# Wider dense products and single-head attention steps in a two-layer hybrid decoder trunk on one NeuronCore

## The chip, the core and the metric

The kernel runs on one core of a Trainium2 chip. The metric is device time in microseconds (us) of one execution of the whole program. TensorE multiplies: it loads a stationary tile and streams a moving tile past it into PSUM, of which a bank here is one tile of 128 x 512 fp32. VectorE and ScalarE do the elementwise work and read PSUM, GpSimd (POOL) does small scalar chains on SBUF, and SyncE (SP) issues most DMA transfers. Every engine runs its own queue of instructions in order.

## What is computed

Two residual layers over 256 tokens of width 2048, with 256 rows of memory; all in fp32. In outline, from the reference:

```python
mem_n = rms_norm(mem, mem_norm_gain)
for i in range(2):
    h = rms_norm(x, norm_gain[i])
    if i == 0:   # 8 NSA heads (3 branches), 4 differential heads, 4 memory heads
        a_q, a_kv, a_g, a_z, b_q, b_k, b_v, b_z, m_q, m_z = split(h @ even_w_in)
        y = concat(nsa(a_q, a_kv, a_g) * silu(a_z), diff(b_q, b_k, b_v) * silu(b_z),
                   memory(m_q, mem_n @ mem_w_kv[0]) * silu(m_z))
    else:        # 12 heads over the top-k tokens of a 16-head indexer, 4 memory heads
        c_q, c_k, c_v, i_q, i_k, i_w, c_z, m_q, m_z = split(h @ odd_w_in)
        y = concat(dsa(c_q, c_k, c_v, i_q, i_k, i_w) * silu(c_z),
                   memory(m_q, mem_n @ mem_w_kv[1]) * silu(m_z))
    x = x + y @ w_out[i]
```

NSA has a compressed branch (15 blocks of 32 tokens through a small MLP), a branch over selected blocks (all of them at this length) and a window branch; each is a masked softmax of its own, and a sigmoid gate weighs them.

## The kernel before

**Numbers in two parts.** Every fp32 operand of a large product is kept as a high part (rounded to fp32r by ScalarE) and a low part (the rest, a VectorE subtraction), and a product is three passes: high x high, low x high, high x low (`passes`). Products of small weight keep plain fp32.

**The weight stream.** `CHUNKS` (L28 to L48) lists the dense products in the order in which their weights are read. A chunk of up to 256 columns comes in four pieces of four k tiles, a wider one in eight pieces of two (`k_tiles`): a piece is 512 KB, 128 x 1024. `emit_raw` loads it through SP's queue up to four pieces ahead; `emit_split` makes `whi` (ScalarE, L189) and `wlo` (VectorE, L190), two pieces ahead, in three buffers each.

**Two kinds of dense product.** `dense_nat` (L221) puts tokens on partitions: the activations are stationary, the weights move, per k tile 3 passes x 2 token blocks. With 256 columns both token blocks share one bank; only memk0 and memk1 are 512 wide. `dense_T` (L247) puts columns on partitions: the weights are stationary, the 256 tokens move, per k tile and column tile three products of 256:

```python
for j, (a, w) in enumerate(((hi, wh), (lo, wh), (hi, wl))):
    T.matmul(outs[ct], w[:, k_, ct * P:(ct + 1) * P], a[:, kt, :], ...)
```

Dense results sit in the pool `pd`, three tiles of one bank; scores in `pS` (two banks), transposes in `pT` (two), attention outputs in `pO` (one).

**The order of the work.** Start: memory keys and values of both layers (memk, memv, memw) beside the norm of x, which generators feed in between (`run_background`, so many steps per weight piece). Layer 0: cmp0, cmp1 and the compression MLP `compress_all` (background, 0.85 steps per piece, its weights through the buffers `raw`), keys and values (ks, vs), then for each of four head pairs `nsa_pair` (L784) and beside them `diff_q`/`diff_pair` (L869, L880), then memory attention (L485), the gates z0 to z7 (`gated`, L952) and the output projection o0 to o7 (L975). Layer 1 (L1000 on): the indexer (ikw, iq), its top-k on VectorE (L1063 to L1074), keys and values, six pairs of DSA heads (L1093 to L1133), memory attention, gates y0 to y7, projection p0 to p7. A framework makes the engines' queues from this program: it takes instructions whose inputs it expects to be ready in the order of their priority, which is the order in the code unless a priority is given, and adds the waits.

In `nsa_pair` two heads share their products with the values (L855 to L863): per branch the first 256 token columns of both heads move as 512, the last 128 of both as 256. `sumsq_heads` takes one ScalarE square with accumulation per token block and head. `gated` reads the gate's product from PSUM and the attention output `oT`, and splits the product of the two into the halves of y.

## Time and profile before

| | |
|---|---|
| three runs | 977.37, 979.40, 981.41 us; median 979.4 us |
| profiled execution | span 976.5 us from first to last instruction; the page lists no further time for it |
| TensorE products | 967.4 us busy (99% of the span), 7801 products |
| TensorE weight loads | 943.2 us busy (97%) |
| VectorE | 642.6 us (66%) |
| ScalarE | 528.7 us (54%) |
| GpSimd | 158.9 us (16%) |
| DMA | 182.40 MB, mean 187 GB/s |

Busy time says in how much of the span an engine had an instruction under way; products overlap one another in TensorE's pipeline, so its busy time can include waits shorter than a product's own duration. The spacing of products (start to start) is what one of them costs.

### The profile page before, as it was taken

The page shows a single profiled execution, that of the slowest core. Times are in us where ns is not written, and L with a number is a line of the kernel's source. Part 1 is how long each engine was busy: PE and PEld are TensorE (multiplying, and loading weights), DVE is VectorE, ACT ScalarE, POOL GpSimd, SP SyncE. Part 2 cuts the span into 40 slices and gives each one's busy share as a digit, 9 for nine tenths or more (in the row PEclk, how much of TensorE's full clock was granted, in tenths as well). Part 3 has the DMA queues.
Part 4 walks back from the last instruction along what each step waited for, and adds up shares of the span by engine and source line. Part 5 has one row for each costly group of instructions (what it writes and reads, how often), then busy time and mean ns, then how long its engine had stood idle before and what let it go on. Part 6 is the DMA issues. An engine that isn't in the chain of part 4 may idle for free.

```text
span 976.5 us, 19895 instructions
## 1 busy us (share of the span) xinstructions
PE 967.4 (99%) x7801; PEld 943.2 (97%) x7801; DVE 642.6 (66%) x1153; ACT 528.7 (54%) x1072; POOL 158.9 (16%) x499
## 2 busy tenths in 40 slices
PE   8999999999999999999999999999999999999998
PEld 6989988899999999999999999999999999999998
DVE  5777854667778766675666667779667667665453
ACT  6756533456676666564454455554466666443332
POOL 0144102223113102200000030021243310000000
PEclk9999999999999999999999999999999999999999
DMA  8765768844444444545677674445654545556772
GB/s 310 253 209 191 238 226 300 286 167 151 143 146 136 133 160 151 171 154 167 205 253 238 192 234 153 148 130 178 194 153 148 156 146 152 171 177 213 218 232 91
DMA packets 55901, 182.40 MB, mean 187 GB/s; under 512 B 6352, under 2 KB 8400, under 8 KB 55808
## 3 DMA queue, kind: packets, MB, share of 16 engines
q1 hardware_dynamic: 54160, 176.77, 55.9%
q0 software_dynamic: 1216, 4.05, 1.3%
q8 instruction: 61, 1.00, 0.4%
q10 hardware_dynamic: 432, 0.32, 0.1%
q14 instruction: 32, 0.26, 0.1%
HBM read 175.88 MB, written 5.24 MB: 185 GB/s over the span
## 4 chain that ended last, share of the span: by engine, by line
PE 96%; DVE 2%; DMA 1%; issue 0%; ACT 0%; SPq 0%; DVEq 0%
PE dn L241 47%; PE dn L262 39%; PE pt L339 2%; PE S L836 1%; PE S L698 1%; PE S L1054 1%; DMA raw<-in_W 1%; PE S L501 1%; DVE wlo L190 1%; PE po L514 1%; PE po L1131 0%; PE S L1117 0%; PE S L908 0%; PE pt L508 0%; DMA raw<-in_w 0%; DVE lo_h L272 0%
## 5 line engine op out<-in xcount | busy, mean ns | idle before, releaser
L190 DVE TENSOR_TENSOR wlo<-raw,whi 128x1024 fp32r<-128x1024 f32 (+3 forms) x305 | 365.0, 1197 | 222.5 <-ACT whi L189 221.0
L189 ACT ACTIVATE whi<-raw 128x1024 fp32r<-128x1024 f32 (+3 forms) x305 | 316.6, 1038 | 315.1 <-PE dn L262 149.4
L241 PE MATMUL dn<-wlo,hi_h 128*128 128x256 f32 (+2 forms) x1024 | 214.3, 287 | 0.0
L241 PE MATMUL dn<-whi,lo_h 128*128 128x256 f32 (+2 forms) x1024 | 213.1, 286 | 0.0
L241 PE MATMUL dn<-whi,hi_h 128*128 128x256 f32 (+2 forms) x1024 | 211.2, 285 | 0.0
L241 PEld LDWEIGHTS dn<-wlo,hi_h 128*128 128x128 f32 x1024 | 161.5, 191 | 5.1 <-issue 3.9
L262 PE MATMUL dn<-hi_h,wlo 128*128 128x256 f32 x576 | 163.6, 284 | 0.7 <-DVE wlo L190 0.7
L262 PE MATMUL dn<-lo_h,whi 128*128 128x256 f32 x576 | 163.7, 284 | 0.0
L262 PE MATMUL dn<-hi_h,whi 128*128 128x256 f32 x576 | 163.6, 284 | 0.0
L241 PEld LDWEIGHTS dn<-whi,lo_h 128*128 128x128 f32 x1024 | 161.4, 191 | 2.1 <-issue 1.2
L241 PEld LDWEIGHTS dn<-whi,hi_h 128*128 128x128 f32 x1024 | 160.7, 191 | 1.5 <-issue 0.8
L262 PE MATMUL dn<-hi_y,whi 128*128 128x256 f32 x512 | 145.0, 283 | 0.0
L262 PE MATMUL dn<-lo_y,whi 128*128 128x256 f32 x512 | 144.9, 283 | 0.0
L262 PE MATMUL dn<-hi_y,wlo 128*128 128x256 f32 x512 | 144.9, 283 | 0.0
L262 PEld LDWEIGHTS dn<-hi_h,wlo 128*128 128x128 f32 x576 | 109.9, 191 | 1.4 <-DVE wlo L190 0.9
L262 PEld LDWEIGHTS dn<-lo_h,whi 128*128 128x128 f32 x576 | 110.1, 191 | 0.0
L262 PEld LDWEIGHTS dn<-hi_h,whi 128*128 128x128 f32 x576 | 110.0, 191 | 0.0
L262 PEld LDWEIGHTS dn<-hi_y,whi 128*128 128x128 f32 x512 | 97.4, 190 | 0.0
L262 PEld LDWEIGHTS dn<-lo_y,whi 128*128 128x128 f32 x512 | 97.4, 190 | 0.0
L262 PEld LDWEIGHTS dn<-hi_y,wlo 128*128 128x128 f32 x512 | 97.4, 190 | 0.0
L372 ACT ACTIVATE E<-E,mn 128x128 f32<-128x128 f32 (+1 forms) x88 | 40.1, 458 | 22.3 <-DVE mn L371 19.5
L241 PE MATMUL dn<-whi,hi_mem 128*128 128x256 f32 (+1 forms) x192 | 47.2, 322 | 2.3 <-ACT hi_mem L430 2.3
(342 smaller groups left out, 1205.7 us busy)
## 6 DMA issues: line engine op xcount, KB each, us to landing
raw<-in_W SPq DMA_DIRECT2D x287, 512.0 KB, 3.6
raw<-in_w SPq DMA_DIRECT2D x16, 512.0 KB, 4.4
raw<-in_W SPq DMA_DIRECT2D x8, 336.0 KB, 3.3
raw<-in_W SPq DMA_DIRECT2D x8, 280.0 KB, 3.3
xs<-in_xT SPq DMA_DIRECT2D x8, 256.0 KB, 5.9
ld<-in_xT SPq DMA_DIRECT2D x8, 256.0 KB, 4.2
x1d<-x POOLq DMA_DIRECT2D x8, 256.0 KB, 4.2
ld<-x1d SPq DMA_DIRECT2D x8, 256.0 KB, 4.2
```

The lines of the kernel that those rows point to most:

```text
L189: state["last"] = (A.activation(hi[:, c], r[:, c], AF.Copy), V.tensor_tensor(lo[:, c], r[:, c], hi[:, c].bitcast(F32), OP.subtract))
L190: V.tensor_tensor(lo[:, c], r[:, c], hi[:, c].bitcast(F32), OP.subtract))
L241: T.matmul(outs[tb], a[:, kt, tb * P:(tb + 1) * P], w[:, k_, :], start=(kt == 0 and j == 0 and (n > 256 or tb == 0)), stop=(kt == KT - 1 a ...
L262: T.matmul(outs[ct], w[:, k_, ct * P:(ct + 1) * P], a[:, kt, :], start=(kt == 0 and j == 0 and (apart or ct == 0)), stop=(kt == KT - 1 and ...
L339: T.transpose(ps[:, b, :], src[:, b * P:(b + 1) * P], ident)
L372: A.activation(E, E, AF.Exp, bias=mn, scale=-1.0, accum_out=sm)
L501: T.matmul(ps_s[:, tb, :], a[:, i, tb * P:(tb + 1) * P], b[:, h, :], start=(j == 0), stop=(j == 2))
L514: T.matmul(po[:, i, :], a[:, mt, h * P:(h + 1) * P], b[:, mt, :], start=(mt == 0 and j == 0), stop=(mt == 1 and j == 2))
L698: T.matmul(ph[l4 * 32:(l4 + 1) * 32, :], blks[j][:, l, :, :].rearrange("p g c -> p (g c)"), wt[:, l4, :], start=(l < 4), stop=(l >= 28), t ...
L836: T.matmul(ps_s[:, :, :n], a[:, i, tb * P:(tb + 1) * P], b[:, g, :, :n], start=(j == 0), stop=(j == 2))
L1054: T.matmul(ps_s[:, :, :n], x[:, b, tb * P:(tb + 1) * P], z[:, :, :n], start=(j == 0), stop=(j == 2))
```

## The change

Dense products of 512 columns wherever two chunks of 256 lay side by side; `dense_T` moves the high and the low part of an activation in one product of 512 columns, into a bank of its own per column tile; attention is written as generators of one head each, of which two run in turn, so many steps per weight piece; a head's output and its gate are multiplied in whichever order they come (`Gated`); memory and differential attention come ahead of NSA; PSUM is two dense tiles of two banks, three banks for the heads and one for preparing queries and keys. The core of the diff:

```diff
-CHUNKS = [("memk0", "mem0", 0, 512), ("memv0", "mem0", 512, 256), ("memw0", "mem0", 768, 256),
...
+CHUNKS = [("memk0", "mem0", 0, 512), ("memv0", "mem0", 512, 512), ("memk1", "mem1", 0, 512), ("memv1", "mem1", 512, 512),
+          ("mq0", "even", 5656, 512), ("cmp0", "even", 1024, 256), ("cmp1", "even", 1280, 256),
+          ("bq", "even", 3608, 512), ("bk", "even", 4120, 512), ("bv", "even", 4632, 512),
+          ("ks", "even", ((1536, 128), (2048, 128), (1664, 128), (2176, 128)), 512),
+          ("vs0", "even", ((1792, 128), (2304, 128), (2560, 24)), 280), ("vs1", "even", ((1920, 128), (2432, 128)), 256),
+          ("aq0", "even", 0, 512), ("aq1", "even", 512, 512)]
...
+CHUNKS += [(f"iq{_i}", "odd", 2560 + 512 * _i, 512) for _i in range(2)]
+CHUNKS += [("mq11", "odd", 5456, 256), ("ck", "odd", 1536, 512), ("cv", "odd", 2048, 512)]
+CHUNKS += [(f"cq{_i}", "odd", 512 * _i, 512) for _i in range(3)]
...
-        pd = ctx.enter_context(tc.tile_pool(name="pd", bufs=3, space=bass.MemoryType.PSUM))
-        pS = ctx.enter_context(tc.tile_pool(name="pS", bufs=2, space=bass.MemoryType.PSUM))
-        pT = ctx.enter_context(tc.tile_pool(name="pT", bufs=2, space=bass.MemoryType.PSUM))
-        pO = ctx.enter_context(tc.tile_pool(name="pO", bufs=1, space=bass.MemoryType.PSUM))
+        pd = ctx.enter_context(tc.tile_pool(name="pd", bufs=2, space=bass.MemoryType.PSUM))
+        pS = ctx.enter_context(tc.tile_pool(name="pS", bufs=3, space=bass.MemoryType.PSUM))
+        pT = pO = pS
...
+        PER_PIECE = 0.9
...
         def run_background():
+            run_attention()
...
+        def step():
+            while len(lines) < 2 and waiting and over.issuperset(waiting[0][2]):
+                lines.append(waiting.pop(0))
+            if lines:
+                line = lines.pop(0)
+                with tc.high_priority(100000):
+                    end = next(line[1], StopIteration) is StopIteration
+                if end:
+                    over.add(line[0])
+                else:
+                    lines.append(line)
+
+        def attended(*numbers):
+            while not over.issuperset(numbers):
+                step()
+
+        def run_attention():
+            steps["due"] += steps["per_piece"]
+            while steps["due"] >= 1:
+                steps["due"] -= 1
+                step()
...
+            ps = pd.tile([P, 2, 512], F32, name="dn")
...
-                    for j, (a, w) in enumerate(((hi, wh), (lo, wh), (hi, wl))):
-                        T.matmul(outs[ct], w[:, k_, ct * P:(ct + 1) * P], a[:, kt, :],
-                                 start=(kt == 0 and j == 0 and (apart or ct == 0)), stop=(kt == KT - 1 and j == 2),
-                                 skip_group_check=True)
+                    cs = slice(ct * P, (ct + 1) * P)
+                    T.matmul(ps[:, ct, :], wh[:, k_, cs], act.both(kt), start=(kt == 0), stop=False, skip_group_check=True)
+                    T.matmul(ps[:, ct, S:], wl[:, k_, cs], act[kt, 0, :], start=False, stop=(kt == KT - 1),
+                             skip_group_check=True)
                 run_background()
-            return ps
+            return ps[:, :, :S], ps[:, :, S:]
...
+            A.activation(junk, v[:, :, off:off + nh * hd], AF.Square)
+            V.tensor_reduce(ssq.rearrange("p (t h) -> p t h", t=2), junk.rearrange("p t (h d) -> p t h d", h=nh), AX.X, OP.add)
...
+        def prep_bank():
+            return pS.tile([P, 512], F32, name="pp", bufs=1)
...
+        class Gated:
...
+            def put(self, c, n, first, second):
+                for seen, run in itertools.groupby(range(n), lambda k: c + k in self.seen):
+                    run = list(run)
+                    k = slice(run[0], run[-1] + 1)
+                    (second if seen else first)(self.oT[:, c + k.start:c + k.stop, :], k)
+                    (self.ready if seen else self.seen).update(c + i for i in run)
+                self.flush()
+
+            def attention(self, c, n, po):
+                self.put(c, n, lambda t, k: A.activation(t, po[:, k], AF.Copy),
+                         lambda t, k: V.tensor_tensor(t, po[:, k], t, OP.mult))
+
+            def release(self, *quarters):
+                self.free |= set(quarters)
+                self.flush()
+
+            def flush(self):
+                for c in range(0, KT, 2):
+                    if {c, c + 1} <= self.ready and c // 4 in self.free:
+                        self.act.open(c // 4)
+                        split(*self.act.parts(c), self.oT[:, c:c + 2, :])
+                        self.ready -= {c, c + 1}
...
+        def total(dst, ph, pl):
+            A.activation(dst, ph, AF.Copy)
+            V.tensor_tensor(dst, dst, pl, OP.add)
...
-        start_background(compress_all(), 0.85)
+        start_background(compress_all(), 0.35)
...
+        def nsa_head(h, q, nsc, pcT, compressed):
+            g, qi = h // 4, h % 4
+            E = tp.tile([P, 2, 3 * P], F32, name="E")
+            sm = sp.tile([P, 2, 2], F32, name="sm")
+            for tb in range(2):
+                n = (tb + 1) * P
+                ps_s = pS.tile([P, 2, S], F32, name="S", tag="one")
+                for j, (a, b) in enumerate(passes(q, kT)):
+                    T.matmul(ps_s[:, :, :n], a[:, qi, block(tb)], b[:, g, :, :n], start=(j == 0), stop=(j == 2))
+                for br in range(2):
+                    softmax_masked(ps_s[:, br, :n], mask_of(tb), nsc[:, tb, qi:qi + 1], E[:, br, part(tb)],
+                                   sm[:, tb, br:br + 1])
+                yield
...
+            for br in range(2):
+                pt = transpose4(E[:, br, :], 3)
+                split(pr[0][:, br, :], pr[1][:, br, :], pt.rearrange("p a b -> p (a b)"))
+                yield
+            while compressed not in over:
+                yield
+            po = pO.tile([P, S], F32, name="po", tag="one")
             for br in range(2):
+                for j, (a, b) in enumerate(passes(vv, [x[:, br] for x in pr])):
+                    T.matmul(po, a[:, 0, g, br, :], b[:, :2 * P], start=(br == 0 and j == 0), stop=False)
+                    T.matmul(po[:, P:], a[:, 1, g, br, :], b[:, 2 * P:], start=False, stop=False)
+            T.matmul(po, vcm[:, g, h % 2, :], pcT[:, qi // 2], start=False, stop=True)
+            out.attention(h, 1, po[:, None, :])
...
+        for g in range(2):
+            v = dense_nat(h0, f"aq{g}")
+            attended(*(heads if g else mem))
+            q, nsc = nsa_q(v)
+            finish_background()
+            pcT = tp.tile([96, 2, S], F32R, name="pcT", bufs=2)
+            comp = attend(nsa_compressed(g, q, nsc, pcT))
+            nsc = nsc.rearrange("p (t h) -> p t h", t=2)
+            nsa += [attend(nsa_head(g * 4 + i, q, nsc, pcT, comp)) for i in range(4)]
...
         for i in range(8):
+            gated(out, f"z{i}", i * 2, h0)
+            if diff in over and i >= 4:
+                out.release(2, 3)
+        attended(diff)
+        out.release(2, 3)
+        attended(*nsa)
+        out.release(0, 1)
...
-            ps = dense_T(y, f"o{i}")
-            V.tensor_tensor(x1[:, c:c + 2, :], ps, xr, OP.add)
+            ph, pl = dense_T(y, f"o{i}")
+            V.tensor_tensor(xr, pl, xr, OP.add)
+            V.tensor_tensor(x1[:, c:c + 2, :], ph, xr, OP.add)
...
+        attended(*mem, *dsa)
+        out.release(0, 1, 2, 3)
```

`attend` appends a generator to `waiting`, with the numbers of those that must be over first; `step` runs one of two `lines` up to its next `yield`. The memory, differential, indexer and DSA heads become generators in the same way; `act.both(kt)` is the high and the low part of a k tile side by side, 512 columns.

## Rows read from the trace of the kernel before

**Rows 1.** The page: busy time, and the granted clock in 40 slices (tenths).

```profile
PE 967.4 (99%) x7801; PEld 943.2 (97%) x7801; DVE 642.6 (66%) x1153; ACT 528.7 (54%) x1072; POOL 158.9 (16%) x499
...
PEclk9999999999999999999999999999999999999999
```

**Rows 2.** The page: the chain that ended last, shares by engine.

```profile
PE 96%; DVE 2%; DMA 1%; issue 0%; ACT 0%; SPq 0%; DVEq 0%
```

**Rows 3.** Windows of 25 us: busy us (instructions) by engine, clock, DMA share, GB/s.

```profile
100.00:125.00 25.00, 24.27 (x203) 24.06 (x202) 20.28 (x50) 12.46 (x19) 2.02 (x5) 1.00 0.69 218
125.00:150.00 25.00, 23.95 (x208) 20.59 (x207) 11.68 (x19) 7.67 (x17) 4.68 (x16) 1.00 0.75 242
300.00:325.00 25.00, 25.00 (x204) 24.61 (x204) 20.15 (x56) 17.83 (x58) 8.79 (x26) 1.00 0.50 156
650.00:675.00 25.00, 25.00 (x211) 24.96 (x210) 22.51 (x61) 12.31 (x22) 6.12 (x19) 1.00 0.54 169
```

**Rows 4.** Groups of TensorE by line and form: shapes, count, busy us, mean ns.

```profile
L241 PE MATMUL dn<-wlo,hi_h 128*128 128x256 f32 x960 | 199.3, 286 | 0.0
...
L262 PE MATMUL dn<-lo_h,whi 128*128 128x256 f32 x576 | 163.7, 284 | 0.0
...
L262 PE MATMUL dn<-hi_y,whi 128*128 128x256 f32 x512 | 145.0, 283 | 0.0
...
L241 PE MATMUL dn<-whi,hi_mem 128*128 128x256 f32 x128 | 26.3, 286 | 0.0
...
L241 PE MATMUL dn<-whi,hi_mem 128*128 128x512 f32 x64 | 20.9, 395 | 2.3 <-ACT hi_mem L430 2.3
```

**Rows 5.** Timeline of TensorE, first 512-wide pair and first 256-wide after 38 pairs.

```profile
14.06 0.62 PE L241 MATMUL dn<-whi,lo_mem 128*128 128x512 f32 x2
...
31.29 0.40 PE L241 MATMUL dn<-whi,hi_mem 128*128 128x256 f32 x2
```

**Rows 6.** The chain in order of time: start us, us, what, products.

```profile
447.78 113.16 PE dn L262 x943
...
658.60 23.27 PE dn L241 x194
```

**Rows 7.** Timeline of all engines near 300 us, in nsa_pair.

```profile
299.75 0.26 PE L798 MATMUL S<-kcT,qh 128*128 128x32 f32 x1
...
299.86 0.26 PE L799 MATMUL S<-kcT,ql 128*128 128x16 f32 x1
...
300.16 0.29 DVE L803 TENSOR_REDUCE c<-S 128x64 f32<-128x128 f32 x1 [0.56 <-PE S L799]
...
300.29 0.28 PE L241 MATMUL dn<-whi,lo_h 128*128 128x256 f32 x1
```

**Rows 8.** Groups of ScalarE by line and form.

```profile
L676 ACT ACTIVATE ew<-dn 128x512 f32<-128x512 f32 x2 | 1.2, 579 | 0.0
```

**Rows 9.** Groups of VectorE by line and form.

```profile
L190 DVE TENSOR_TENSOR wlo<-raw,whi 128x1024 fp32r<-128x1024 f32 x287 | 350.8, 1223 | 201.1 <-ACT whi L189 199.6
...
L272 DVE TENSOR_TENSOR prl<-pt,prh 128x384 fp32r<-128x384 f32 x16 | 8.5, 552 | 5.2 <-ACT prh L271 5.1
...
L371 DVE CUSTOM_DVE_ANT_0 E<-S,cst,nsc 128x256 f32<-128x256 f32 x16 | 7.2, 475 | 1.2 <-PE S L836 1.2
...
L371 DVE DVE_READ_ACCUMULATOR2_ANT mn<- 128x1 f32 x72 | 5.9, 82 | 0.0
...
L980 DVE TENSOR_TENSOR x<-dn,ld 128x512 f32<-128x512 f32 x8 | 5.5, 692 | 6.1 <-PE dn L262 6.1
...
L371 DVE CUSTOM_DVE_ANT_0 E<-S,cst,nsc 128x128 f32<-128x128 f32 x16 | 5.2, 346 | 0.3 <-PE S L836 0.2
...
L378 DVE TENSOR_SCALAR E<-E,sm 128x128 f32<-128x128 f32 x20 | 5.0, 282 | 0.2
...
L935 DVE TENSOR_TENSOR l<-l,ro 128x1024 f32<-128x1024 f32 x1 | 1.2, 1226 | 2.4 <-POOL ro L299 2.4
```

**Rows 10.** Timeline: a wait for a load of the compression, and the kernel's end.

```profile
126.68 0.42 PE L698 MATMUL S<-raw,l 128*32 128x256 f32 x4 [1.05 <-DMA raw<-in_w]
...
973.14 0.42 DVE L1151 TENSOR_TENSOR row<-dn,ld 128x256 f32<-128x256 f32 x1 [1.01 <-PE dn L262]
```

More of the change, by code (lines that the diff above doesn't have):

```diff
@@ L214, in start_background, with attend @@
             background.append([gen, per_piece, 0.0])
+        waiting, lines, over = [], [], set()
+        steps = {"per_piece": 0.0, "due": 0.0, "number": 0}
+        def attend(gen, *after):
+            steps["number"] += 1
+            waiting.append((steps["number"], gen, after))
+            return steps["number"]
+        def step():
[17 more added lines that the diff above has]
+                step()
         def finish_background():
@@ L400, in big_pair, with __init__, open, both @@
-        def big_pair(slot, name):
-            return Halves(f"hi{slot}", f"hi_{name}"), Halves(f"lo{slot}", f"lo_{name}")
+        class Act:
+            def __init__(self, slot, name, now=True):
+                self.slot, self.name, self.t = slot, name, {}
+                if now:
+                    for i in range(4):
+                        self.open(i)
+            def open(self, i):
+                if i not in self.t:
+                    self.t[i] = big.tile([P, 4, 2, S], F32R, name=f"{self.name}{i}", tag=f"{self.slot}{i}")
+            def __getitem__(self, key):
+                kt, part, c = key
+                return self.t[kt // 4][:, kt % 4, part, c]
+            def both(self, kt):
+                return self.t[kt // 4][:, kt % 4].rearrange("p l s -> p (l s)")
+            def parts(self, c, n=2):
+                return [self.t[c // 4][:, c % 4:c % 4 + n, i] for i in range(2)]
@@ L440, in token_rstd @@
         def token_rstd(acc, out):
-            ps = pT.tile([P, 2], F32, name="pt")
+            ps = pT.tile([P, 2], F32, name="pt", tag="one")
             for tb in range(2):
@@ L690, in compress @@
         def compress(j):
-            ph = pS.tile([P, 256], F32, name="S")
+            ph = pS.tile([P, 256], F32, name="S", tag="one")
             for pc in range(8):
@@ new lines, in trunk @@
+        dqs = diff_q(dense_nat(h0, "bq"))
+        v = dense_nat(h0, "bk")
+        attended(*mem)
+        bkT = diff_k(v)
+        v = dense_nat(h0, "bv")
+        bv = kp.tile([P, 2, 512], F32, name="bv", tag="memv0")
+        ob = kp.tile([P, 2, 4, P], F32, name="ob", tag="memv1")
+        A.activation(bv, v, AF.Copy)
+        heads = [attend(diff_head(h, *dqs, bkT, bv, ob)) for h in range(4)]
+        diff = attend(diff_out(ob), *heads)
+        gate = kp.tile([P, 2, 24], F32, name="gate")
@@ new lines, in trunk, with gated @@
+        nsa = []
+        for g in range(2):
+            v = dense_nat(h0, f"aq{g}")
[6 more added lines that the diff above has]
+            nsa += [attend(nsa_head(g * 4 + i, q, nsc, pcT, comp)) for i in range(4)]
+        def gated(out, name, c, h, rb=None):
+            ph, pl = dense_T(h, name)
+            z = tp.tile([P, 1024], F32, name="rp1", bufs=1)[:, :512].rearrange("p (c s) -> p c s", c=2)
+            total(z, ph, pl)
@@ L1042, in trunk @@
-        mem_attention(1, v, 80, 0, memkT, memv, oT, 12, r1)
-        for ic in range(4):
-            v = dense_nat(h1, f"iq{ic}")
-            qn, qn3 = nat_tile()
-            rope_apply(qn3, v[0][0], 4, 64, c64, s64)
-            q = q_tiles()
-            split_T(q, transpose4(qn))
-            for b in range(2):
+        for tb in range(2):
+            pt = transpose4(kn[:, tb], 1, prep_bank())
+            for c in range(2):
+                o = slice(c * 64, (c + 1) * 64)
+                split(kI[0][o, c, block(tb)], kI[1][o, c, block(tb)], pt[o, 0])
@@ L1134, in trunk @@
-        mem_attention(1, dense_nat(h1, "mq11"), 0, 2, memkT, memv, oT, 14, r1)
-        y = big_pair("B", "y1")
+        scores = []
+        for ic in range(2):
+            v = dense_nat(h1, f"iq{ic}")
+            if ic:
+                attended(*mem)
+            qn = nat_tile()
+            rope_apply(qn, v, 8, 64, c64, s64)
+            scores.append(attend(index_scores(ic, transposed(qn)), *scores))
+        chosen = [attend(index_top(tb), *scores) for tb in range(2)]
+        v = dense_nat(h1, "mq11")
@@ new lines, in trunk @@
+        attended(scores[0])
+        qm = mem_q(1, v, 0, 2, r1)
+        mem = [attend(mem_attention(*qm, h, 2 + h, memkT, memv, out, 14 + h)) for h in range(2)]
+        v = dense_nat(h1, "ck")
+        kn = nat_tile()
+        ssq = sumsq_heads(v, 4, P, kn)
+        rk = rsq(ssq, 8, 1.0 / P, EPS, "rk", r=r1)
+        rope_apply(kn, v, 4, P, nk[0][:, :, 0], nk[1][:, :, 0])
+        knh = kn.rearrange("p t (c d) -> p (t c) d", c=4)
+        V.tensor_tensor(knh, knh, rk[:, :, None].to_broadcast([P, 8, P]), OP.mult)
```

742 lines of the change are left out of this document (324 added, 418 removed), and 3 rows, old and new, of the table CHUNKS.

## Prediction, before the changed kernel was run

> **What bounds the kernel now.** Busy times first [rows 1]: TensorE is busy 99% of a 976.5 us span, at the full granted clock (2.4 GHz) in every slice; VectorE has 66%, ScalarE 54%. A busy TensorE can still hide waits, so I went on to the chain of waits [rows 2]: 96% of the span is TensorE work that follows on TensorE work. The table of windows [rows 3] shows the same in attention: 650 to 675 us has 211 products in 25.00 us, though VectorE is at 22.51. Last, the spacing. From 447.78 to 560.94 us, 943 products 256 wide run in 113.16 us, 120.0 ns each, and at 658.60 us 194 take 23.27 us, 119.9 ns [rows 6]: nothing is missing between them. So only what TensorE issues counts, and a wait counts only where it becomes TensorE's.
>
> A product's price has two parts. 512 wide, the timeline has 76 products from 14.06 to 31.29 us: 17.23 us, 226.7 ns each [rows 5]. Twice the columns thus cost 106.7 ns more, 0.417 ns a column (one per cycle at 2.4 GHz), and **13.3 ns** come with every product at either width. The dense products are 3 x (960 + 128) 256 wide in dense_nat, 3 x (576 + 512) in dense_T, and 192 of 512 [rows 4].
>
> **The change, step by step.** *1. dense_nat, 512 wide.* memv+memw twice, mq, bq, bk, bv, ks, aq (two), iq (two), ck, cv, cq (three): 16 pairs of 256-wide chunks of 96 products become single chunks of 96. 16 x 96 = 1536 products fewer, the columns stay: 1536 x 13.3 ns = 20.5 us.
>
> *2. dense_T.* 34 chunks (2 cmp, 8 each of z, o, y, p), 32 pairs of column tile and k tile each. Three 256-wide products (360 ns) become one of 512 over high and low part together and one of 256 (346.7 ns): 34 x 32 = 1088 fewer, 14.5 us. 512 and 256 in alternation isn't in the trace; each is, at the same 13.3 ns, so I take the sum. Ends: nothing, and 14.5.
>
> Steps 1 and 2: 2624 products, **-35.0 us**. The Trainium skill, "TensorE: Matmul & The Clock Gate", section Back-to-back issue gap, gives an isolated gap of N/2.4 + 2.5 ns. By it 2624 products would be worth 6.6 us, not 35.0, an estimate that speaks against the change; this trace shows 13.3 ns [rows 5, 6] and decides.
>
> *3. Single heads.* Scores, transposes and the DSA, memory and differential products keep their shapes. In nsa_pair, L855 to L863 issue 6 products of 512 and 6 of 256 (2.08 us); two single heads issue 12 of 256 and 12 of 128. High/low products 128 wide are not in the trace: below, 66.7 ns if columns rule; above, 226.7, as a 512-wide one. The nearest rows are products of 32 and 16 columns that still lie 0.11 us apart [rows 7], so I take 110: 2.76 us. Four pairs: **+2.7 us**, between 0.6 and 8.
>
> *4. Vector work added.* dense_T now leaves two sums in PSUM. cmp, z, y: 18 ScalarE copies (0.58 us) [rows 8] and 18 VectorE adds (0.69); o and p: one more add each (16) [rows 9]. Sums of squares go from ScalarE with accumulation to one 1024-wide square and a VectorE reduction (about 1.2 us as the 1024-wide row, a dozen). Some 23 + 15 us on VectorE, hidden while TensorE has split weights: VectorE's free third covers it, except in the stretch of step 6 and in the last chunk, where a second 256-wide add (0.42 us) follows the final product [rows 10]: **+0.4**.
>
> *5. Weights of the compression.* compress_all advances 0.35 instead of 0.85 per piece, so its 16 loads on SP's queue spread over some 46 pieces. Today one wait of TensorE there, 1.05 us, is for such a load [rows 10]; the window 125 to 150 us is short by as much, the one before it by 0.73 [rows 3]: **-1.8**. Ends: 0, since that wait can return elsewhere, and -4 if the loads also delay products inside the busy time.
>
> *6. New order, generators, gating.* The steps carry priority 100000, so their instructions stand ahead of later dense work on each engine; today the same happens by program order, and TensorE goes on with dense products while VectorE starts on the scores [rows 7]. What can be late is VectorE. From aq1 to z3 it must do: 24 pieces x 1.223 = 29.4; two query preparations (reduction, rope, two low parts) 2 x 6.4 = 12.8; eight heads x (two maxima of 0.346 and two of 0.475 with reads of 0.082, two rescales near 0.28, two low parts of 0.552, small ones 0.33: 3.97) = 31.8, and 3.4 for eight multiplications by the gate; compressed branch about 8; four gates 7.5. Together 93 us [rows 9]. TensorE needs 96 x 226.7 ns = 21.8 (aq1), 4 x 32 x 346.7 ns = 44.4 (four z), 8 x 3.2 for the heads (3 products of 512, 10 of 256, 12 transposes and products of 128 at 0.11) and 6 for preparations: 98. 95% is above the 90% of 650 to 675 us [rows 3], so splits come late. Ends: 0, and 18 if VectorE fills only to the 81% of 300 to 325 us, the busiest stretch of attention [rows 3] (93/0.81 = 115, less 98). I take **+5**, nearer to the fuller window, since z4 to z7 leave room.
>
> PSUM: dense tiles drop from three of one bank to two of two. A 512-wide chunk lasts 21.8 us and its readers need about 6, a dense_T chunk 11.1 and about 1.3; I cost it at nothing unless VectorE is late (step 6). DMA volume is unchanged.
>
> **Sum.** -35.0 + 2.7 + 0.4 - 1.8 + 5 = -28.7. Against the profiled span of 976.5: 947.8. The median of the three runs shown, 979.4, is 2.9 above that span: **951 us**.
>
> **Rivals.** *A. VectorE becomes the bound* from aq1 to z3 (18 us instead of 5) and, weaker, in the layer-1 attention. For it: 95% demand, no slack for an engine that waits in order. Against: 90% passes today without a gap. 951 + 13 = 964, to 974.
>
> *B. Hand-over after the gates.* After z7 and y7 the code drains what is left of the heads, then splits the gated output over scratch that the heads used (release). With 0.9 steps a piece, aq1 and z bring 36 of the 44 NSA steps; eight remain, four deep on two lines. If the engines' order follows the written order, each link costs a round of score, maximum, exponent and transpose of about 3 us: 12 us there, little after y (its 36 steps fit): 963. Against: dependencies end with z3.
>
> *C. Slower.* The place is TensorE's queue, in order, in both layers: score, transpose and product of a head share three PSUM banks, and a head's last product holds its bank until the gate of its columns has been read. 138 steps are issued (74 and 64). If a step's product waits at the head of the queue for the step before (maximum and exponent, above 1 us unhidden, half covered by the second line), the dense products behind it stand still. From 0.24 us a step (33 us) it cancels the gain; at 0.4 it gives 946 + 55 = about 1001. Against: dense products have no part in these waits, and there are none today.
>
> *D. Less than promised.* dense_T's mixed pair saves nothing, or most of the fixed part belongs to the loading of the stationary tile and comes back per column: 951 + 14.5 = 966 for the first; 951 + 28 = 979, no change, for the second. Against: [rows 5] has the same fixed part at 512 wide. By the Trainium skill's 2.5 ns (same page and section as above) it would end at 951 + 28.4 = 979 too.
>
> **Chances.** Forecast 0.57, A 0.19, B 0.08, C 0.08, D 0.08 (half of it no change). Over 0.5% (4.9 us, about what a measurement can tell) faster is below 974.5: 0.57 + 0.08 + 0.04 and A but for its tail give 0.86; same 0.06; slower 0.08. The forecast's own range is 940 (nothing late, 128-wide products cheap, loads fully hidden) to 960; A, B and half of D stretch it to 971.
>
> **What would show it.** Right: TensorE products fall by about 2580 (2624 less, 48 more); a 512-wide dense product spaced 226.7 ns and a dense_T pair of 346.7; windows still at 25.00 us; VectorE near 70% overall and above 90% in the aq1-z3 stretch. Wrong: dense_T pairs at 360 (D); gaps before dense products that wait for the low part of a split (A); a hole after the last z (B); TensorE idle before scores or transposes throughout (C). 128-wide products far from 110 ns would shift the sum by up to 6 us.

## The result, and the profile after

The changed kernel takes **970.47 us** (median, 969.62 to 973.47), the kernel before, run beside it, 979.58 (977.37 to 981.41). The ratio is 0.9916, 95% interval 0.9891 to 0.9941: faster, by about 9 us, where the prediction had 28.4 (951 us), a range of 940 to 960 for its own forecast and 971 with its rivals. The profiled execution took 969.85 us, its span 968.1.

The page of the changed kernel: busy times, 40 slices of 24.2 us, and the chain that ended last.

```profile
PE 950.3 (98%) x5225; PEld 807.5 (83%) x5225; DVE 669.6 (69%) x1137; ACT 516.8 (53%) x853; POOL 130.1 (13%) x345
...
PE   8989999999999999999899999999999999999998
...
PEclk9999999999999999999999999999999999999999
...
PE 89%; DVE 4%; POOL 2%; DMA 2%; issue 1%; ACT 1%; SPq 0%; ACTq 0%; DVEq 0%; POOLq 0%
```

Beside [rows 1] TensorE has 2576 products fewer, which is 2624 less and 48 more, as forecast. The chain is 89% TensorE instead of 96% [rows 2]. The windows say where the rest came in.

Windows of 25 us (busy us and instructions of PE, PEld, DVE, ACT, POOL; then clock, DMA share, GB/s):

```profile
50.00:75.00 25.00, 22.34 (x98) 18.12 (x97) 16.38 (x24) 11.79 (x18) 18.57 (x52) 0.93 0.55 176
375.00:400.00 25.00, 24.27 (x154) 21.47 (x153) 19.77 (x53) 17.65 (x42) 0.00 (x0) 1.00 0.43 135
450.00:475.00 25.00, 21.43 (x134) 18.80 (x133) 19.35 (x46) 17.16 (x38) 0.00 (x0) 1.00 0.39 116
650.00:675.00 25.00, 25.00 (x124) 20.88 (x123) 24.08 (x69) 12.93 (x23) 3.39 (x12) 1.00 0.47 148
850.00:875.00 25.00, 22.13 (x136) 19.16 (x135) 20.45 (x39) 18.31 (x36) 0.00 (x0) 1.00 0.46 144
```

The same windows of the kernel before, where 375 to 400 us is also at 25.00:

```profile
50.00:75.00 25.00, 25.00 (x136) 21.57 (x136) 18.60 (x28) 13.53 (x22) 11.93 (x34) 1.00 0.62 210
450.00:475.00 25.00, 25.00 (x211) 25.00 (x210) 15.05 (x16) 11.11 (x14) 0.00 (x0) 1.00 0.52 170
850.00:875.00 25.00, 25.00 (x210) 25.00 (x210) 16.43 (x18) 11.37 (x14) 0.00 (x0) 1.00 0.60 189
```

650 to 675 us is still full, with VectorE at 24.08 of 25: the window in which VectorE was fullest in [rows 3] lost nothing. The short ones are the start (50 to 75), one place among the gates (375 to 400), and the two ends of the gates, where z hands over to o (450 to 475) and y to p (850 to 875). All of them were full before. What TensorE waited for:

```profile
PE pp L354 <- DVE nat L525: 2.7, 1, 2.7
PE dn L277 <- DVE y L287: 2.2, 2, 1.3
PE dn L277 <- DVE rp L460: 1.8, 2, 1.1
PE pt L354 <- DVE prl L287: 1.8, 1, 1.8
...
PE S L1198 <- DVE mn L382: 0.9, 1, 0.9
```

(us in total, times, longest.) The 512-wide products cost what was forecast. The timeline of dense_nat, 512 wide, at the start, and the spacing of dense_T's pairs through o and through p (product, count, durations, first and last start):

```profile
30.25 1.07 PE L262 MATMUL dn<-whi,mem 128*128 128x512 f32 x4
...
43.85 1.07 PE L262 MATMUL dn<-whi,mem 128*128 128x512 f32 x4
```

```profile
L277 PE MATMUL dn<-y,whi x199: 395/398/403, 479.7 to 549.7; 128*128 128x512 f32 x199
```

```profile
L277 PE MATMUL dn<-y,whi x160: 392/394/395, 889.8 to 944.9; 128*128 128x512 f32 x160
```

From 30.25 to 43.85 us ten rounds of six products take 13.60 us, 226.7 ns each, as in [rows 5]. In p, 159 pairs of one 512-wide and one 256-wide product take 55.1 us, 346.5 ns, the forecast 346.7; in o 198 pairs take 70.0 us, **353.5**.

So I priced every product of both traces by the prediction's rule (0.417 ns a column and 13.3, at least 110 ns for small ones; the compression's 128 products of 32 stationary columns at the 71 ns that they average before) and took the sum from the time between the first and the last product. What is left is waiting, slower spacing and lower clock:

```
us            products  priced | left, by stretch of the span
                               |  0-50  50-100 100-325 325-450 450-500 500-750 750-850 850-900 900-end    sum
before            7801   959.7 |   7.2     0.3     5.5    -0.2     0.0    -0.3    -0.3     0.0     0.0   12.0
changed           5225   927.5 |   6.2     5.5     8.5     2.1     4.8     2.2     1.1     4.1     0.0   34.5
1 dense_T cut     6313   942.0 |   5.9     5.3    10.4     0.0    -0.1     1.0    -0.2    -0.1     0.0   22.4
2 dense_nat cut   6761   948.0 |   5.8     2.8     4.6     0.9     9.7    -0.3     0.7     0.3     0.0   24.5
3 both cut        7849   962.4 |   6.4     2.9     4.5    -0.1    -0.1    -0.3    -0.4    -0.1     0.0   12.9
4 start           5225   927.5 |   5.9     0.9    10.6     2.1     5.9     1.0     1.3     5.5     0.0   33.0
5 rate 1.3        5225   927.5 |   6.2     4.9     9.7     6.4     3.7     1.1     1.1    10.0     0.0   43.1
6 order of o0     5225   927.5 |   5.9     5.4     8.2     2.1     0.1     1.0     1.2     4.4     1.1   29.5
7 order of pairs  5225   927.5 |   6.5     5.2     9.0     1.2     4.4     1.3     0.6     8.1     0.3   36.7
8 two buffers     5225   927.5 |   7.9     4.3     9.6     0.8     9.4     2.3     1.1     7.6     1.3   44.2
9 scratch apart   5225   927.5 |   6.1     5.6     9.1     2.1     0.1     1.0     1.1     4.5     0.0   29.6
11 together       5225   927.5 |   5.8     0.8    10.1     2.1     0.1     1.1     2.3     3.3     0.0   25.5
```

Priced products fell by 32.2 us (forecast: 35.0 less 2.7). What is left grew by 22.5. The difference, less 1.2 us of a longer tail after the last product starts, is the 8.4 us between the two spans. **The saving is there; two thirds of it went into waiting, slower spacing and lower clock.** The lower rows are the experiments, by number.

### The profile page after: what moved, and what is told of

Read it like the earlier page. It is cut to its first block, busy times and chain, and to the rows that moved or that the text cites. A ratio compares the mean times of both kernels' runs of the same rounds, so it can differ in the third digit from the quotient of the medians.

```text
span 968.1 us, 14359 instructions
## 1 busy us (share of the span) xinstructions
PE 950.3 (98%) x5225; PEld 807.5 (83%) x5225; DVE 669.6 (69%) x1137; ACT 516.8 (53%) x853; POOL 130.1 (13%) x345
## 4 chain that ended last, share of the span: by engine, by line
PE 89%; DVE 4%; POOL 2%; DMA 2%; issue 1%; ACT 1%; SPq 0%; ACTq 0%; DVEq 0%; POOLq 0%
PE dn L262 41%; PE dn L277 25%; PE dn L278 13%; DVE wlo L186 1%; PE pp L354 1%; PE S L747 1%; DMA raw<-in_W 1%; PE pt L354 1%; PE S L1131 1%; PE S L983 1%; PE po L1003 1%; PE po L567 1%; ACT whi L185 1%; PE S L550 1%; DMA xs<-in_xT 1%
## 5 line engine op out<-in xcount | busy, mean ns | idle before, releaser
L262 PE MATMUL dn<-whi,h 128*128 128x512 f32 (+3 forms) x1152 | 295.7, 372 | 0.0
L262 PEld LDWEIGHTS dn<-whi,h 128*128 128x128 f32 x1152 | 203.9, 188 | 38.1 <-issue 4.3
L277 PE MATMUL dn<-h,whi 128*128 128x512 f32 x576 | 206.9, 398 | 1.8 <-DVE rp L460 1.8
L277 PE MATMUL dn<-y,whi 128*128 128x512 f32 x512 | 179.7, 397 | 2.2 <-DVE y L287 2.2
L262 PE MATMUL dn<-wlo,h 128*128 128x512 f32 (+3 forms) x576 | 169.5, 373 | 0.0
L278 PE MATMUL dn<-h,wlo 128*128 128x256 f32 x576 | 163.7, 284 | 0.0
L278 PE MATMUL dn<-y,wlo 128*128 128x256 f32 x512 | 142.8, 279 | 0.0
L277 PEld LDWEIGHTS dn<-h,whi 128*128 128x128 f32 x576 | 108.2, 188 | 24.9 <-DVE rp L460 2.2
L262 PEld LDWEIGHTS dn<-wlo,h 128*128 128x128 f32 x576 | 103.4, 188 | 18.6 <-issue 1.6
L278 PEld LDWEIGHTS dn<-h,wlo 128*128 128x128 f32 x576 | 108.8, 189 | 0.7
L262 PEld LDWEIGHTS dn<-wlo,mem 128*128 128x128 f32 x128 | 24.2, 190 | 5.7 <-DVE wlo L186 0.6
```

The costliest lines, as they stand in the source:

```text
L262: T.matmul(ps[:, tb, :n], act[kt, part, tb * P:(tb + 1) * P], w[:, k_, :], start=(kt == 0 and j == 0), stop=(kt == KT - 1 and j == 2), ski ...
L277: T.matmul(ps[:, ct, :], wh[:, k_, cs], act.both(kt), start=(kt == 0), stop=False, skip_group_check=True)
L278: T.matmul(ps[:, ct, S:], wl[:, k_, cs], act[kt, 0, :], start=False, stop=(kt == KT - 1), skip_group_check=True)
```

## The experiments

The theories at the outset: *holes* (the products are worth their price, the rest was lost to waits that have nothing to do with width), and *width* (the shorter dense work itself brings the waits, and undoing it closes them). The kernel before took 979.6 to 980.4 us (medians) beside every one of them, so that times can be set side by side; ratios are to the kernel before.

**1. dense_T cut back.** The 512-wide product of high and low part becomes two of 256, into the same halves, for the same readers. (This kernel and those of runs 2 and 3 leave part of a chunk's first pass out of the sum; number, shape, operands and order of the instructions are as described.)

```diff
-T.matmul(ps[:, ct, :], wh[:, k_, cs], act.both(kt), start=(kt == 0), ...)
+for i in range(2):
+    T.matmul(ps[:, ct, i * S:(i + 1) * S], wh[:, k_, cs], act[kt, i, :], start=(kt == 0), ...)
```

> The changed kernel with dense_T's 512-wide product cut back into two of 256 (1088 products more, readers unchanged): step 2 undone alone. Theory H (holes): the products are worth what the shorter ones save, and the missing gain of the whole change sits in waits of TensorE elsewhere (63 to 72 us, 466 to 472, 858 to 874). Then this is slower than the changed kernel (970.5 us) by 14.5 us at the forecast 13.3 ns a product, by about 9 us if the pairs that the changed kernel shows at 353 instead of 347 ns cost 6.7 ns of that: 979 to 985 us. Rival W (width): the wide form itself brings the waits, so undoing it closes them and gives most of the products back: within 5 us of 970.5.

Measured: 972.19 us, ratio 0.9921 (0.9903 to 0.9940), 1.7 us above the changed kernel, which the intervals do not tell apart. By price its products cost 14.5 us more (942.0 against 927.5 in the table), and 12.1 us of what is left went. The same windows:

```profile
450.00:475.00 25.00, 25.00 (x213) 25.00 (x212) 19.19 (x32) 16.00 (x28) 0.00 (x0) 1.00 0.52 168
...
850.00:875.00 25.00, 25.00 (x212) 25.00 (x211) 19.92 (x32) 16.48 (x29) 0.00 (x0) 1.00 0.48 154
```

Both hand-overs are full. The eight gates of z take 121.6 us (347.1 to 468.7) instead of 116.0 (344.8 to 460.8), and the last NSA head's product lies at 465.1 us, before their end, where in the changed kernel it lies at 470.6, 9.8 us behind it. *Width* was right on the time, *holes* on the price of a product: both ends of one thing.

**2. dense_nat cut back** to 256 columns in the 16 merged chunks.

```diff
-T.matmul(ps[:, tb, :n], act[kt, part, tb * P:(tb + 1) * P], w[:, k_, :], ...)
+for c in ((slice(0, 256), slice(256, 512)) if n == 512 and name[:4] != "memk" else (slice(0, n),)):
+    T.matmul(ps[:, tb, c], act[kt, part, tb * P:(tb + 1) * P], w[:, k_, c], ...)
```

> The changed kernel with each 512-wide dense_nat product of the 16 merged chunks cut into two of 256 over the same banks (1536 products more, order and readers unchanged): step 1 undone alone. Theory H: slower than the changed kernel by 1536 x 13.3 ns = 20.5 us, about 991 us. Rival W: the long chunks bring the waits, and with twice the products there is more to cover them: less than half of it, below 981 us.

Measured: 978.57 us, ratio 0.9984 (0.9969 to 0.9998): 8.1 us above the changed kernel, for 20.5 us of products by price: *width*'s side of the mark. What is left shrank at the start by 2.7 us, at 100 to 325 us by 3.9, at the hand-over to p by 3.8. The one to o did not close: its waits are those of the changed kernel (1.9, 0.7 and 1.5 us), and a lower clock, 0.91 and 0.81 in its two windows, takes it to 9.7.

**3. Both cut back**, by the two edits above.

> The changed kernel with both kinds of product cut back (2624 products more): what is left of the change is its order, generators, gating and banks. The first two runs gave 972.2 and 978.6 us, 1.7 and 8.1 above the changed kernel. Theory T (each saving is given back only where a chain is exposed, at ends of stages): the sum of both or somewhat more, as the chains that one cut closes need no second one: 980 to 992 us. Rival O (the other parts cost the missing gain): with no product saved the kernel would be slower than the kernel before by those 20 us: about 1000 us. A value at or below 980 says that the other parts cost nothing.

Measured: 983.34 us, ratio 1.0044 (1.0028 to 1.0060). What is left is 12.9 us, the 12.0 of before again, and the priced products stand 2.7 above before, the single heads' smaller products. So order, generators, banks and gates cost 4 to 5 us by themselves: these 2.7 (2.0 as measured), 2.6 at the start (2.9 against 0.3) and 1.3 of a longer tail, less 1.7 that the other stretches gave back. Rival *other parts* is out: the rest of the lost time comes only with the saved products. Of 34.9 us of products (2624 x 13.3 ns) the kernel keeps 983.3 - 970.5 = **12.9**.

**4. The start.** In the changed kernel's program the product memv0 comes behind the memory's norm and its keys. In TensorE's queue its 96 products run first all the same (30.2 to 52.3 us), then those of memk1; the transposes of memk0's keys stand behind 45 of these. The timeline of the changed kernel there:

```profile
64.48 0.20 POOL L301 TENSOR_TENSOR mkf<-mkf,rmk 128x8 f32<-128x8 f32 x1
64.71 1.23 DVE L525 TENSOR_TENSOR nat<-nat,mkf 128x1024 f32<-128x1024 f32 x1 [2.36 <-POOL mkf L301]
...
65.99 0.66 PE L354 MATMUL pp<-cst,nat 128*128 128x128 f32 x4 [2.65 <-DVE nat L525]
...
67.29 1.91 PE L262 MATMUL dn<-whi,mem 128*128 128x512 f32 x4
69.00 1.05 PE L262 MATMUL dn<-wlo,mem 128*128 128x512 f32 x2
```

```profile
66.00:69.00 3.00, 3.00 (x12) 2.40 (x12) 2.20 (x2) 1.55 (x2) 2.61 (x5) 0.68 0.31 57
69.00:72.00 3.00, 3.00 (x12) 2.40 (x10) 0.06 (x1) 0.73 (x1) 2.20 (x12) 0.75 0.82 289
72.00:75.00 3.00, 3.00 (x17) 2.54 (x16) 3.00 (x5) 1.31 (x3) 1.02 (x2) 1.00 0.54 131
```

A transpose at the head of TensorE's queue waits for GpSimd's chain of small operations, and the rest of memk1's products, which need none of it, stand behind it. That chain ends at 64.7 us; in the kernel before it ended at 58.9, ahead of the transposes (60.5). After the wait the granted clock is 0.68 and 0.75 in two windows of 3 us, 1.7 us of full speed lost: four products from 67.29 to 69.00 take 427 ns each, the 1.2 GHz level, instead of 227.

```diff
+ps = dense_nat(memA, "memv0")
 finish_background()
 token_rstd(accm, rm)
 mem_k(mk, rm, keep_k)
-start_background(load_x(), 1.4)
-ps = dense_nat(memA, "memv0")
+start_background(load_x(), 1.7)
```

> The changed kernel with the product memv0 put ahead of the memory's norm, its keys and the loads of x, as in the kernel before (x then comes beside memk1 and memv1 at 1.7 steps a piece instead of 1.4). Theory H: TensorE's wait at 63 to 66 us for the normalized memory keys and the stretch at half clock behind it go, and the time falls by 5 to 7 us, to 963.5 to 965.5. Rival (moved): the same chain of norms on GpSimd then makes the normalized x late, TensorE waits as long before mq0, and the time stays within 2 us of 970.5.

Measured: 968.41 us, ratio 0.9885 (0.9866 to 0.9903), 2.1 us less than the changed kernel, the intervals overlapping. The place is right, and so is half of the rival. The chain ends no earlier (66.9 us), but the transposes now stand behind 71 products of memk1, at 68.3 us, and do not wait: 4.6 us of the start went. 2.1 came back in mq0, whose products now wait for the normalized x, and 2.5 at the two hand-overs, whose waits were no longer but were now followed by a lower clock (0.93 in both windows). The start and mq0:

```profile
50.00:75.00 25.00, 24.77 (x114) 20.24 (x113) 17.23 (x25) 14.47 (x21) 10.91 (x34) 1.00 0.57 201
100.00:125.00 25.00, 23.43 (x107) 18.73 (x106) 21.05 (x55) 13.46 (x21) 1.68 (x3) 1.00 0.72 223
```

**5. More attention per piece**, `PER_PIECE` 1.3 instead of 0.9.

> The changed kernel with 1.3 instead of 0.9 attention steps per weight piece: the heads are over before z7 and y7. Theory H: the pacing leaves steps for after the gates, where TensorE has nothing to cover them; the holes at 466 to 472 us (about 4 us) and 858 to 874 us (about 4) shrink to half or less, and the time falls by 4 to 7 us, to 963.5 to 966.5. Rival V (VectorE late): VectorE cannot take more steps a piece beside the splits, dense products wait for the low parts from aq1 on, and the time is 970 us or more.

Measured: 980.38 us, ratio 1.0004 (0.9986 to 1.0022), 10 us slower than the changed kernel. The hand-over to o fell only from 4.8 to 3.7 us, the one to p rose from 4.1 to 10.0, and a hole of 3.1 us opened among the gates (392 us). TensorE's waits in this run:

```profile
PE dn L277 <- DVE rp L460: 6.4, 2, 5.3
PE pt L354 <- ACT rp L459: 3.1, 1, 3.1
```

In the longest, before p0, VectorE's timeline has splits of y, a gate and a weight split ahead of the sum named there. The remedy was wrong, and so was the theory of the pace behind it: with 1.3 steps a piece the last NSA head's product lies at 472.8 us, later than with 0.9 (470.6) and still 6.1 behind the gates' end. That the steps' priority over dense work is why more of them hurt fits this, but no run took the priority away.

**6. The hand-over to o.** The timeline of the changed kernel, TensorE and VectorE alone:

```profile
463.69 1.15 PE L354 MATMUL pt<-cst,E 128*128 128x128 f32 x9
464.86 1.22 DVE L186 TENSOR_TENSOR wlo<-raw,whi 128x1024 fp32r<-128x1024 f32 x1 [0.86 <-ACT whi L185]
466.01 0.55 DVE L287 TENSOR_TENSOR prl<-pt,prh 128x384 fp32r<-128x384 f32 x1
...
466.61 0.55 PE L354 MATMUL pt<-cst,E 128*128 128x128 f32 x3 [1.77 <-DVE prl L287]
...
472.22 0.50 PE L277 MATMUL dn<-y,whi 128*128 128x512 f32 x1 [1.28 <-DVE y L287]
```

The first quarter of o0 is through. Then come twelve transposes of the last two heads, of which the last three wait for a bank that a low part (466.01) has yet to read, and that low part stands behind a weight split that was itself not ready (0.86 us idle). (No run gave the heads another bank.) The second quarter of o0 needs these heads' columns of y; the third and fourth do not, but come behind it. The edit multiplies them first:

```diff
+QUARTERS = {"o0": (0, 2, 3, 1)}
...
-for q in range(4):
-    wh, wl = weights(first[name] + q)
+for i, q in enumerate(QUARTERS.get(name, (0, 1, 2, 3))):
+    wh, wl = weights(first[name] + i)
```

> The changed kernel with the four weight pieces of o0 in the order 0, 2, 3, 1: the quarter of y that the last two NSA heads fill is multiplied last instead of second, so two quarters of dense work (5.5 us) lie beside these heads. Theory T (exposed tail): the gaps of 450 to 475 us (4.4 us in the changed kernel, waits of 1.94, 0.68 and 1.49 us) are the last heads' chain with nothing behind it on TensorE's queue; they shrink below 1.5 us and the time falls by 3 to 5 us, to 965.5 to 967.5. Rival R (heads late): the heads themselves come too late, TensorE then waits before the last quarter of o0 instead, and the time stays within 1.5 us of 970.5.

Measured: 964.97 us, ratio 0.9855 (0.9837 to 0.9872): 5.5 us less, for an order of four pieces. What is left at 450 to 500 us fell from 4.8 to 0.1, and 1.2 more went behind it, where o's pairs have the closer spacing (below). No wait remains:

```profile
450.00:475.00 25.00, 25.00 (x160) 22.41 (x159) 18.65 (x45) 16.91 (x38) 0.00 (x0) 1.00 0.41 126
```

**7. The spacing of dense_T's pairs.**

```diff
 for n in range(8):
     T.matmul(ps[:, ct, :], wh[:, k_, cs], act.both(kt), ...)
-    T.matmul(ps[:, ct, S:], wl[:, k_, cs], act[kt, 0, :], ...)
+    if n % 2 == 0:
+        continue
+    for n_ in (n - 1, n):
...
+        T.matmul(ps[:, ct, S:], wl[:, k_, cs], act[kt, 0, :], ...)
```

> The changed kernel with dense_T's products in another order: both column tiles' 512-wide products first, then both 256-wide ones (512, 512, 256, 256 instead of 512, 256, 512, 256). Theory P (phase): the alternation falls into a pattern of 353.3 us per thousand pairs in most stages and 346.7 in others by where it started, not by what runs beside it; another order has another pattern, and the pairs come at one price in all undisturbed stages. If that is 346.7 ns, some 800 pairs save 5 us. Rival B (beside): the slower spacing comes from the work of the other engines beside it; then o stays at 353 and p at 347, and the time within 1 us of 970.5. The order has no part in the sum of the products otherwise.

Measured: 973.15 us, ratio 0.9933 (0.9912 to 0.9955), 2.7 us above the changed kernel, the intervals overlapping. The views of o and p in this run, and the same two of the run before:

```profile
L277 PE MATMUL dn<-y,whi x203: 393/395/398, 479.6 to 550.0; 128*128 128x512 f32 x102
```

```profile
L277 PE MATMUL dn<-y,whi x159: 393/395/398, 889.8 to 944.8; 128*128 128x512 f32 x159
```

```profile
L281 PE MATMUL dn<-y,whi x203: 390/392/397, 479.6 to 549.7; 128*128 128x512 f32 x102
```

```profile
L281 PE MATMUL dn<-y,whi x157: 395/398/403, 889.7 to 944.8; 128*128 128x512 f32 x157
```

Grouped, o and p both stand at 348 ns a pair (202 in 70.4 us, 158 in 55.0): one price, as *phase* said, though not 346.7. In the run before it is o that has 347 and p 353, the reverse of the changed kernel, and in runs 2, 4, 5 and 9 to 11 both have 347. The closer spacing even has the busier VectorE beside it (475 to 500 us: 20.8 us in the run before, 16.4 in the changed kernel). That speaks against the other engines' work as the cause; in o and p the alternation settles at one of two spacings. What makes it settle is open. The time did not fall because the queues moved as well: before p0 TensorE waits 3.1 us here, and 850 to 900 us has 8.1 left instead of 4.1.

**8. Two buffers for the gates' scratch.** At 388.9 and 859.96 us a dense product of the gates waits for `total` (L460) to have read the banks it needs, and at 860 us the timeline of the changed kernel reads (VectorE and TensorE):

```profile
858.09 1.22 DVE L186 TENSOR_TENSOR wlo<-raw,whi 128x1024 fp32r<-128x1024 f32 x1
...
859.22 0.68 DVE L460 TENSOR_TENSOR rp<-rp,dn 128x512 f32<-128x512 f32 x1
...
859.96 0.50 PE L277 MATMUL dn<-h,whi 128*128 128x512 f32 x1 [1.11 <-DVE rp L460]
```

```diff
-z = tp.tile([P, 1024], F32, name="rp1", bufs=1)[:, :512]...
+z = nat_tile(256)
```

> The changed kernel with the gates' scratch z taken from the two buffers of the query preparation instead of one buffer of its own. Theory D (dense banks): the waits of dense products behind the sum of the two PSUM parts (0.89 us at 388.9, 1.27 us at 859.96) come because a gate's total must wait for the gate before to be through with its one scratch, and so holds the two banks; with two they go, and the time falls by 1 to 4 us. Rival V (VectorE late anyway): the total stands behind splits and head steps in VectorE's queue; the waits stay, and the time within 1 us of 970.5.

Measured: 976.14 us, ratio 0.9969 (0.9956 to 0.9982). The waits for L460 went, as *dense banks* said, and the time rose by 5.7 us, which neither theory had: TensorE's wait for the splits of y became

```profile
PE dn L277 <- DVE y L287: 7.0, 3, 3.4
```

instead of 2.2 us. The gates run closer together (z takes 112.3 us instead of 116.0), but the last NSA head ends later, at 475.4 instead of 470.6 us. On VectorE the last heads' maxima, which lay before 458.3 us in the changed kernel, now lie up to 464.1, after z7, and the low part of y's first quarter behind them:

```profile
464.07 1.28 DVE L287 TENSOR_TENSOR y<-oT,y 128x512 fp32r<-128x512 f32 x2
...
464.81 0.79 PE L277 MATMUL dn<-y,whi 128*128 128x512 f32 x1 [3.41 <-DVE y L287]
```

Why the queues came out in that order is open.

**9 to 11. The hand-over to p, and all together.** In layer 1 the scratch of the DSA heads lies where y will be, so that y could not be split before the last head's last product. The edit puts their values elsewhere, and the index scores and biases beside k0 (with the order of o0 kept); then the start of run 4 is added, then x at 2.2 steps a piece.

```diff
-v1 = r[:, 512:1024]
+v1 = [cp.tile([P, P], F32, name=f"v1{i}", tag=t) for i, t in enumerate(("dqa", "dqb", "dka", "dkb"))]
...
-v0 = [r[:, 1024 + i * 512:1536 + i * 512] for i in range(2)]
...
+r = region("B", 2, "v01", F32R)
+v0 = [r[:, i * 512:(i + 1) * 512] for i in range(2)]
```

> The kernel with o0's pieces in the order 0, 2, 3, 1 (965.0 us), and in layer 1 the DSA values in other scratch: v0 in the region of the third quarter of y, v1 in tables of layer 0 that are no longer needed, the index scores and biases beside k0. The first two quarters of y1 then no longer wait for the last head's products with v0 and v1. Theory T: the wait before p0 (1.06 to 1.19 us at the hand-over from y7 to p0, and half clock where it follows) is the chain last product, gate, split of y; with the splits of the first quarters out of it, the wait goes and the time falls by 1 to 2 us, to 963 to 964. Rival S (splits late): ScalarE and VectorE have the splits of y behind the last gates in any case; the wait stays as long, and the time within 0.7 us of 965.0.

> The kernel of the run before in this list with memv0 also put ahead of the memory's norm (x at 1.7 steps a piece). The start alone gave 968.4 us beside 970.5 for the changed kernel: the waits at 63 to 66 us went, and 1.9 us of waits for the normalized x came at 113 to 117 us. Theory T (the gains lie at separate places and add): 2 us less than the run before, 961 to 962. Rival: the start moves everything behind it against the pacing, and the gains of the other two places are lost again: 965 or more.

> As the run before, with x at 2.2 instead of 1.7 steps a piece: the normalized x is ready some four pieces (11 us) earlier. Theory T: the waits at 113 to 117 us go as well and the time falls by another 1 to 2 us, to about 960. Rival V: VectorE, at 21 of 25 us there, cannot take the faster pace; splits come late, TensorE waits before dense products between 75 and 110 us, and the time is no less than that of the run before.

Measured: 963.88 us, ratio 0.9831 (0.9806 to 0.9855); 961.82, 0.9812 (0.9786 to 0.9838); **960.18, 0.9791 (0.9766 to 0.9816)**. In the first the wait of p0 for y is gone from the list of waits, but after the waits at 853 to 855 us, for maxima and L460, the clock now fell (0.83 from 850 to 860 us), so that the window as a whole kept 4.5 us; the 1.1 us by medians is within the intervals, and the trace alone shows the wait gone. The start added as expected (2.1 us), and the faster x took the waits in mq0 away, though 1.6 us by medians is again within the intervals; a wait for a load of the compression came back instead (1.2 us at 272.6, the wait that step 5 had taken off). The windows of the last:

```profile
50.00:75.00 25.00, 24.86 (x114) 20.31 (x114) 18.21 (x28) 14.50 (x21) 11.08 (x34) 1.00 0.57 201
100.00:125.00 25.00, 24.80 (x113) 20.09 (x112) 21.64 (x55) 13.90 (x22) 1.67 (x3) 1.00 0.73 232
...
450.00:475.00 25.00, 25.00 (x157) 22.35 (x156) 18.75 (x40) 17.65 (x35) 0.00 (x0) 1.00 0.44 137
850.00:875.00 25.00, 24.46 (x135) 21.39 (x136) 20.74 (x35) 15.57 (x26) 0.00 (x0) 0.93 0.40 130
```

This version is 10 us faster than the changed kernel and 20 faster than the one before.

**12. Two buffers on top.**

> The kernel that has all three edits (start at 2.2 steps a piece, order of o0, scratch apart; 960.2 us) with two buffers for the gates' scratch. Alone, two buffers took the waits near 389 and 858 us away and cost 5.7 us in all, by waits before o0 (3.6 us) and p0 (2.6 us). Theory T: these two came because the last heads ended after the last gates with nothing beside them; here other quarters of y lie beside them, so the waits near 385 and 850 us (0.9, 1.0 and 1.3 us, and half clock after) go without that price: 956 to 958 us. Rival H (hand-over moved): the wait before o0's first quarter (for the scores of the last head and the splits behind them) stays, about 3.5 us, and the time is 960 us or more.

Measured: 966.72 us, ratio 0.9857 (0.9836 to 0.9877). The rival: the first quarter of o0 waits for splits of y that stand behind four maxima on VectorE, 3.4 us, and again at its end.

```profile
PE dn L281 <- DVE y L291: 6.0, 2, 3.4
```

## Why the prediction was wrong, and where it was right

The forecast was 951 us, and 970.5 lies outside its own range (940 to 960). That it lies inside the range that the rivals stretched to 971 is luck: several losses came together that no rival had.

*Steps 1 and 2, the products (-35.0): right.* 2624 fewer, 226.7 ns at 512 wide; rival D is out. By the Trainium skill ("TensorE: Matmul & The Clock Gate", Back-to-back issue gap) they would have been worth 6.6 us, an estimate from its 2.5 ns; the traces keep 13.3 ns a product at 256 and at 512 columns. Only the mixed pair was mis-sized: the 993 pairs of the changed kernel that no wait interrupts average 350.7 ns instead of 346.7, some 4 us over 1088.

*Step 3, single heads (+2.7): right.* The 96 products of 256 and 128 columns take 11.0 us from start to start, the 48 that they replace took 8.7: 2.3. *Step 4's tail (+0.4)* measured 1.2. *Step 5 (-1.8) did not come:* the waits at 109 and 127 us are gone, but the compression's 16 groups of eight small products were torn into 20 by dense work between them (128 products: 9.1 us before, 11.7 after, next start to next start), and 100 to 325 us has 8.5 us left instead of 5.5.

*Step 6 (+5) is the one that failed,* with the sentence before the sum that cost the banks at nothing (waits for them took 0.9 us at 388.9 and 1.3 at 860). Step 6 looked for lateness where VectorE is busiest, aq1 to z3, and put the work of all eight heads there, 95% of VectorE's time. But at 0.9 steps a piece these 24 pieces bring 21.6 of the 44 NSA steps, by the count that rival B itself uses; VectorE had 62.4 of 82.6 us there (319.4 to 402 us, 76%), and the wait at 388.9 is the only one that came. It took for granted that everything hidden today stays hidden under dense work that is 35 us shorter. The runs show the opposite at both ends: 4.8 and 4.1 us are left at the two hand-overs; cut dense_T or both products back and both close (runs 1 and 3), cut dense_nat alone and the one to p closes (run 2), and the order of four pieces closes the one to o (run 6). The chains were rival B's, which had 0.08 and one hand-over at 12 us; it came at both, at less each. "Dependencies end with z3" was no reason against it, since heads run beside all eight gates; what sets where they end is open, as a faster pace did not move them (run 5).

*Not in the sum at all:* the start. The diff moves memv0 behind the norm and mem_k in the program, and the keys' transposes came to stand in TensorE's queue before GpSimd's chain was through: 5.2 us with the lower clock, 2.6 of it even with all products cut (run 3). And no step allowed for the clock, which no slice of before shows below 9.

Together: 8.9 us at the hand-overs, 5.2 at the start, 4 of pairs, 2.6 of the compression and 0.9 among the gates make up 21.6 of the 22.5 that what is left grew by.

Rival A (VectorE the bound) did not come: aq1 to z3 stood at 76%, and 650 to 675 us runs at 24.08 of 25 and is full. Rival C did not: behind the start TensorE waits at a few places (389, 467 to 472, 858 to 860 and 874 us), not per step.

## What to carry to other kernels

Where one engine is busy 99% of the span, as TensorE was here, the latency of the other chains is hidden, and the views of before did not show how narrowly. Before counting a saving on that engine, list the places where its queue must wait for a chain (start, hand-overs, last heads), and ask of each how much dense work lies beside it now and after; the saving in that work can be given back there first. The cheapest cure is order: put beside the exposed chain the work that doesn't depend on it (four pieces of o0: 5.5 us).

## What the runs showed of the hardware

- After waits of TensorE between 1 and 5 us the granted clock sometimes fell to the 1.2 GHz level for some microseconds and sometimes not: the same two waits at the end of y (1.0 and 1.3 us) were followed by 1.00 in their window in the changed kernel and by 0.93 in run 4, 1.7 us of full speed lost. A wait can cost about its own length again.
- Pairs of 512- and 256-wide products settled in o and p at 346.5 or 353.5 ns and stayed there; in the changed kernel the first eight pairs of o stood at 347, those behind the wait at 353. In the order 512, 512, 256, 256 it is 348 in both stages.
- 512-wide products cost 226.7 ns from start to start (60 in 13.60 us), where two of 256 cost 240.0. The 13.3 ns a product hold through both layers: with all products cut back (run 3), what is left by that price is 12.9 us, beside 12.0 in the kernel before.
